# Row maxima of the attention scores by way of DRAM instead of TensorE

## The chip, the cores and the metric

The kernel runs on one core of one Trainium2 chip. The metric is the time of one execution on the device in microseconds (us), the median of several runs. TensorE is PE here (PEld is its weight load), VectorE is DVE, ScalarE is ACT, GpSimd is POOL, and SyncE is SP, whose queue issues nearly all DMAs.

## The reference

One layer of a decoder trunk over 2048 positions of width 1024, all in float32. After a norm, one input projection feeds an mLSTM group of four heads and an attention group (MLA) of eight heads; one output projection joins them, and a feed-forward part of width 4096 follows. The change lies in the attention of the eight heads:

```python
sc = jnp.einsum('bhqd,bkhd->bhqk', qblk, kf) * scale      # 96 wide: 64 plain, 32 rotary
sc = jnp.where(kpos[None, :] <= qpos[:, None], sc, -jnp.inf)
p = jax.nn.softmax(sc, axis=-1)
out = jnp.einsum('bhqk,bkhd->bqhd', p, vf)
```

## The kernel before

The program works through four stages: norm and input projections with the mLSTM (up to about 520 us of the profile), attention (about 520 to 965), the output projection (from about 964), and the feed-forward part (to the end).

In attention each head `h` goes through four blocks `qb` of 512 queries. For every block there are two passes. The first, `maxima` (L1548), finds a maximum for each query: a single rough product of queries and keys per 128 queries and up to 512 keys (`mm`, L1569, tile `m`, 512 columns wide where no mask falls), a maximum over the keys on DVE (`red`, L1574 and L1576, tile `mp`), and one more reduction over the pieces (`top_`, L1595), which leaves a tile `mx` of 128 partitions by 4 columns: the maximum of query `128 j + p` on partition `p`, column `j`. The second pass, `step` (L1615), makes the scores transposed, keys on partitions and queries along the row, in three products (`scores`, L1623, through the helper lines L245 to L247, tile `S`), takes their exponential on ACT (L1633, L1637), forms the low part of it on DVE or POOL (L1641, tile `pl`), and multiplies with the values (L1654, L1652, L1657, tile `o`).

The maximum has to be subtracted from scores that lie with the queries along the row. That is done inside the product: queries and keys have 96 rows, and a 97th, partition 96 of the tiles `QK0` (even heads) and `QK1` (odd heads), holds the negated maximum beside the queries and 1 beside the keys. To bring the maxima from partitions onto that row, `rows_` (L1597) runs four matmuls per block with one column of `mx` as weights and a 128x128 identity as the moving operand (L1600, tile `mt`, 1 partition by 512), and `put` (L1602) copies that row with a factor of -1 from PSUM to partition 96 on ACT (L1603). The row of ones is loaded once per tile `QK` from the input `edge` (L1473).

The order of PE, ACT, DVE and POOL is fixed in advance. A planner (`Plan`, L125) takes every operation with an estimated duration, its dependencies, its buffers and a key of urgency, places them greedily in time, and the instructions are written and pinned in that order (`pin`, L255). The first score of a block depends on `o_m[h, qb]`, the operation that leaves the row on partition 96. The DMAs on SP's queue are not pinned; the framework orders them, and SP issues them strictly one after another, waiting in front of each for what it needs. In attention SP's queue carries the loads of the next heads' queries and keys (L1523, L1525), the values (L1538), and for every finished block the store of its output (L1737) and of its sums (L1738), the load of the sums across partitions (L1742) and the store of their reciprocals (L1748).

The names in the orders and rows below read: `m5_3_3_3` is head 5, block 3, queries 3, keys 3; `mx5_3` the maxima of head 5, block 3; `S5_2_5` the scores of head 5, block 2, key tile 5. The number after the last underscore counts buffers.

Of the kernel before, what the change touches and what calls it, by code (L numbers as in the profile page):

```python
# [10 lines left out]
F32 = mybir.dt.float32  # L11
F32R = mybir.dt.float32r
I32 = mybir.dt.int32
BF16 = mybir.dt.bfloat16
AF = mybir.ActivationFunctionType
# [3 lines left out]
P = 128  # L19
SEQ = 2048  # L20
DM = 1024
KD = DM // P
TB = 512
# [4 lines left out]
NH = 8  # L28
# [9 lines left out]
TB_ = 1  # L38
TR_ = 1
EARLY = ()  # L40
EKEY = -165.0
EGAP = 1.5
LOL = 20.0
# [77 lines left out]
def f32(ap):  # L121
    return ap.bitcast(F32)
# [114 lines left out]
def trunk(ctx: ExitStack, tc: tile.TileContext, x, xT, pos, wu, wout, wup, wdn, cols, rows, consts, edge, out, dbg=None):  # L237
# [3 lines left out]
    vec, act, pool, pe = nc.vector, nc.scalar, nc.gpsimd, nc.tensor  # L241
    dma = nc.sync.dma_start
# [26 lines left out]
    dram = ctx.enter_context(tc.tile_pool(name="dram", bufs=1, space=DRAM))  # L269
# [16 lines left out]
    trep = [dram.tile([P, 2, TB], F32, tag=f"trep{b}", name=f"trep{b}") for b in range(NB)]  # L286
    trigd = dram.tile([64, SEQ], F32, tag="trigd", name="trigd")
    sumd = dram.tile([NH, SEQ], F32, tag="sumd", name="sumd")
    recd = dram.tile([NH, SEQ], F32, tag="recd", name="recd")
    x1d = out  # L290
    x1Td = dram.tile([DM, SEQ // 2], F32, tag="x1Td", name="x1Td")
# [4 lines left out]
    pl = Plan()  # L296
# [1110 lines left out]
    a2 = av = ar2 = pq = pS = po = onecol = maskneg = maskb = identb = None  # L1407
    pm = []
    QK, Qh, Ql, Kh, Kl = ([None, None] for _ in range(5))
# [42 lines left out]
    o_s1 = pl.op("Z", 0, switch1, pl.groups["e2"], -KEYA)  # L1452
    o_s2 = pl.op("Z", 0, switch2, unit_ops + [o_s1], -KEYA)
    o_s3 = pl.op("Z", 0, switch3, pl.groups["in"] + [o_s2], -KEYA)
    pl.group = "prep"
    for name, bufs, when in (
        ("q", 1, o_s1), ("m", 2, o_s2), ("S", SB_, o_s3), ("o0", 1, o_s3), ("o1", 1, o_s3), ("t", TB_, o_s3), ("th", 1, o_s3), ("tl", 1, o_s3), ("ph", HB_, o_s3), ("p", 1, o_s3), ("pl", LB_, o_s3), ("ot", 1, o_s3), ("ou", 1, o_s3),
        ("mp", 4, o_s1), ("mx", 2, o_s1), ("rsm", 2, o_s3),
    ):
        pl.ring(name, bufs, when)  # L1460

# [18 lines left out]
    blocks, first, start_of = [], {}, {}  # L1480
# [32 lines left out]
    o_kr, o_k, o_q, o_m, o_sc, o_pv, o_v = {}, {}, {}, {}, {}, {}, {}  # L1513
# [34 lines left out]
    def maxima(h, qb, keys):  # L1548
        s = h % 2
        mp = {}  # L1550
        reds = []

        def ring(i):
            return "q" if (h, qb) in EARLY or i % 3 == 2 else "m"

        def bank(i, name):
            return (pq if ring(i) == "q" else pm[0]).tile([P, TB], F32, tag=ring(i), name=name)

        def piece(j, kb, key):
            n = TB if kb < qb else (j + 1) * P  # L1560
            t = {}
            i = len(reds)

            def mm():
                if "t" not in mp:
                    mp["t"] = a2.tile([P, 4, 4], F32, tag="mp", name=f"mp{h}_{qb}", bufs=4)
                q0 = qb * TB + j * P
                t["p"] = ps = bank(i, f"m{h}_{qb}_{j}_{kb}")
                pe.matmul(ps[:, :n], Qh[s][0:96, q0 : q0 + P], Kh[s][0:96, kb * TB : kb * TB + n], start=True, stop=True)  # L1569

            def red():
                ps = t["p"]
                if kb < qb:
                    vec.tensor_reduce(mp["t"][:, j, kb : kb + 1], ps, axis=AX.X, op=ALU.max)  # L1574
                else:
                    vec.tensor_tensor_reduce(  # L1576
                        out=ps[:, :n], in0=ps[:, :n], in1=maskneg[:, 512 - n :], op0=ALU.add, op1=ALU.max, scale=1.0, scalar=NEG,
                        accum_out=mp["t"][:, j, kb : kb + 1],
                    )

            head = not reds
            a = pl.op("PE", n / 2.4 + (56 if n == P else 15), mm, [o_q[h, qb][0], o_k[h, kb][0], o_kr[s, kb], o_const[s]], key, take=(ring(i), "mp") if head else (ring(i),))
            if head:
                mp["op"] = a
            reds.append(pl.op("DVE", n / 0.96 + (148 if kb < qb else 285), red, [a, o_mask] if head else [a, o_mask, mp["op"]], key - 3, free=[(ring(i), a)]))

        todo = [(j, kb) for j in range(4) for kb in range(qb + 1)]
        for (j, kb), key in zip(todo, keys):
            piece(j, kb, key)
        t = {}  # L1590
        key = keys[-1] - 3

        def top_():
            t["m"] = a2.tile([P, 32], F32R, tag="mx", name=f"mx{h}_{qb}")[:, 0:4]
            vec.tensor_reduce(t["m"], mp["t"][:, :, 0 : qb + 1], axis=AX.X, op=ALU.max)  # L1595

        def rows_():  # L1597
            t["p"] = bank(len(reds), f"mt{h}_{qb}")
            for j in range(4):
                pe.matmul(t["p"][0:1, j * P : (j + 1) * P], t["m"][:, j : j + 1], identr, start=True, stop=True)  # L1600

        def put():  # L1602
            act.activation(Qh[s][96:97, qb * TB : (qb + 1) * TB], t["p"][0:1], AF.Copy, scale=-1.0)  # L1603

        a = pl.op("DVE", 80, top_, reds, key, take=("mx",), free=[("mp", mp["op"])])
        b = pl.op("PE", 4 * 75, rows_, [a, o_const[s]], key, take=(ring(len(reds)),), free=[("mx", a)])
        war = [o_sc[n] for n, (hh, q, _) in enumerate(blocks) if (hh, q) == (h - 2, qb)]
        o_m[h, qb] = pl.op("Activation", 585, put, [b] + war, key, free=[(ring(len(reds)), b)])

    acc, totals, tiles_of, lows = {}, {}, {}, []  # L1610
# [163 lines left out]

    early = [x for x in EARLY for _ in range(4 * x[1] + 4)]
    for i, x in enumerate(early):
# [26 lines left out]
    n = GT * P  # L1803
# [829 lines left out]
    for c in range(NCH):  # L2633
        ws = []
        for e in range(2):
            p = 2 * c + e
# [23 lines left out]
def prepare(inputs):  # L2660
    a = {k: np.asarray(v) for k, v in inputs.items()}
    x = np.ascontiguousarray(a["x"].reshape(SEQ, DM))
    w = a["w_in"][0]

    def unit(c):
        return c.reshape(KD, P, P).transpose(1, 0, 2).reshape(P, KD * P)

    kr = w[:, 1928:1960]
    z = np.zeros((DM, 56), np.float32)
    misc = np.concatenate([w[:, 1536:1544], z, kr, kr[:, 16:], kr[:, :16]], axis=1)  # L2670
    us = [unit(misc)]
    us += [unit(w[:, i * P : (i + 1) * P]) for i in range(4)]
    v = w[:, 512:1024].reshape(4, 2, P, 512)
    us += [v[j].transpose(1, 0, 2).reshape(P, 1024) for j in range(4)]
    us += [unit(w[:, 1024 + i * P : 1024 + (i + 1) * P]) for i in range(4)]
    us += [unit(w[:, 1544 + i * P : 1544 + (i + 1) * P]) for i in range(3)]
    ukv = a["w_ukv"][0].reshape(P, NH, 128)
    us.append(np.concatenate([ukv[:, :, :64].reshape(P, 512), ukv[:, :, 64:].reshape(P, 512)], axis=1))
    uq = a["w_uq"][0].reshape(2, P, NH, 96)
    us.append(uq[..., :64].reshape(2, P, 4, P).transpose(1, 2, 0, 3).reshape(P, 1024))  # L2680
    rope = uq[..., 64:].reshape(2, P, 2, 4, 2, 16).transpose(1, 2, 0, 4, 3, 5).reshape(P, 512)
    us.append(np.concatenate([rope, np.zeros((P, 512), np.float32)], axis=1))
    wu = np.ascontiguousarray(np.stack(us))
    wup = np.ascontiguousarray(a["w_up"][0].reshape(KD, P, DFF // P, P).transpose(2, 1, 0, 3).reshape(DFF // P, P, DM))

    def cv(v):
        return v.reshape(-1, P).T

    conv = a["conv_w"][0].reshape(4, 4, P).transpose(2, 1, 0).reshape(P, 16)
    cols = np.concatenate(  # L2690
        [conv, cv(a["conv_b"][0]), cv(a["norm_pre_mix"][0]), cv(a["ml_head_norm"][0]), cv(a["q_norm"][0]), cv(a["kv_norm"][0])], axis=1
    )
    rows = np.concatenate([a["b_gates"][0], a["norm_post_mix"][0], a["norm_pre_mlp"][0], a["norm_post_mlp"][0]])[None]
    consts = np.zeros((P, K_N), np.float32)
    consts[:, K_ID : K_ID + P] = np.eye(P)
    r = np.arange(P)
    consts[:, K_MASK + 384 : K_MASK + 512] = np.where(r[None, :] <= r[:, None], 0.0, NEG)
    consts[:, K_MASKT : K_MASKT + P] = np.where(r[None, :] >= r[:, None], 0.0, NEG)
    inv = np.array(INV_FREQ_BITS, np.uint32).view(np.float32)
    consts[:, K_INV] = inv[r % 16]  # L2700
    consts[:, K_NOT] = r != 64
    consts[:, K_OFF] = np.array([0.25, 0.25, 0.5, 0.0])[(r % 64) // 16]
    return {
        "x": x,
        "xT": np.ascontiguousarray(x.T),
        "pos": np.ascontiguousarray(a["positions"].reshape(1, SEQ)),
        "wu": wu,
        "wout": np.ascontiguousarray(a["w_out"][0]),
        "wup": wup,
        "wdn": np.ascontiguousarray(a["w_down"][0]),  # L2710
        "cols": np.ascontiguousarray(cols),
        "rows": np.ascontiguousarray(rows),
        "consts": consts,
        "edge": np.stack([np.ones(SEQ, np.float32), np.zeros(SEQ, np.float32)]),
    }


# [20 lines left out]
```

## Time and profile before

| | before |
|---|---|
| median of 3 runs | 2419.19 us (2416.09 to 2419.89) |
| profiled execution, its own time | 2418.22 us |
| its span in the trace | 2415.7 us |
| granted TensorE clock, mean | 0.994 |
| matmuls in the trace | 11135 |
| matmuls at L1600 (tile `mt`) | 128, 4 for each of 32 blocks |
| row copies at L1603 | 32, median 586 ns |

The span is what the trace covers, from the first instruction to the last; 2.5 us of the execution's time lie around it. A matmul's row gives its start and a duration; successive matmuls overlap, so how much time one takes from PE is read from the distance between starts. A line of a timeline gives the start in us, the duration in us, engine, source line, operation, result and operands, shape, and in brackets the idle time ahead of it with what ended it. SPq is SP's queue; its rows are issues of DMAs, not their landing. A line of waits reads: engine and line, then who was waited for, then the total in us, the number of times, and the longest one.

### The profile page before, as it was taken

Reading aid. Unit: us, or ns where it says so; the run is one execution under the profiler, and the core shown is the slowest. Engines: PE = TensorE matmul, PEld = TensorE weight load, DVE = VectorE, ACT = ScalarE, POOL = GpSimd, SP = SyncE. Lnnn points to the kernel's source line nnn. Section 1 sums busy time; section 2 is a strip of 40 time slices with the busy share of each in tenths; the row PEclk is TensorE's granted clock in tenths of the full one; section 3 lists DMA queues with packets and bytes.
Section 4 is the critical chain, followed back from the end, with each engine's and each line's share of the span. In section 5 each row is a group of like instructions: output and inputs, shape, how many; then the busy total and the mean of one; then the engine's idle time right before and its main releaser. Section 6 shows DMA issues by size and latency. Waiting matters only on the chain.

```text
span 2415.7 us, 34327 instructions
## 1 busy us (share of the span) xinstructions
PE 2372.5 (98%) x11135; PEld 1907.3 (79%) x11135; DVE 1722.8 (71%) x3125; ACT 1363.1 (56%) x2646; POOL 814.0 (34%) x697
## 2 busy tenths in 40 slices
PE   9999999999999999999999999999999999999997
PEld 7787777777777777788888888888888888888885
DVE  6865665658888887646866687766675677676778
ACT  5645454437788777544666556755665343443454
POOL 2634343428888888432000000000000322322346
PEclk9999999989999999999999999999999999999999
DMA  7697979887222321567877697755664435445448
GB/s 280 219 320 229 336 239 337 271 208 168 72 57 54 80 60 26 157 202 249 258 213 227 195 327 225 210 171 166 184 214 144 159 127 183 129 136 169 133 136 167
DMA packets 341308, 449.21 MB, mean 186 GB/s; under 512 B 34908, under 2 KB 227432, under 8 KB 341128
## 3 DMA queue, kind: packets, MB, share of 16 engines
q1 hardware_dynamic: 337192, 440.16, 58.6%
q0 software_dynamic: 3936, 6.87, 2.0%
q8 instruction: 87, 1.43, 0.2%
q14 instruction: 93, 0.76, 0.1%
HBM read 295.97 MB, written 153.05 MB: 186 GB/s over the span
## 4 chain that ended last, share of the span: by engine, by line
PE 53%; DVE 1%; DMA 1%; issue 0%; ACT 0%; SPq 0%; POOL 0%; DVEq 0%; ACTq 0%; POOLq 0%
PE op L245 1%; PE op L246 1%; PE op L247 1%; PE d_4X L2510 1%; PE d_3X L2512 1%; PE d_5X L2512 1%; PE d_4X L2512 1%; PE d_1X L2512 1%; PE d_1X L2511 1%; PE d_2X L2511 1%; PE d_3X L2511 1%; PE d_2X L2512 1%; PE d_4X L2511 1%; PE d_5X L2511 1%; PE d_5X L2510 1%; PE d_1X L2510 1%
## 5 line engine op out<-in xcount | busy, mean ns | idle before, releaser
L2548 POOL TENSOR_TENSOR y<-vd_0X,y 128x512 f32<-128x512 f32 x7 | 10.3, 1475 | 726.1 <-ACT vd_0X L2545 726.1
L1668 POOL TENSOR_TENSOR t<-t,ph 128x512 f32<-128x512 f32 (+1 forms) x192 | 213.0, 1110 | 17.8 <-ACT ph L1633 7.4
L1633 ACT ACTIVATE ph<-S 128x512 fp32r<-128x512 f32 (+1 forms) x320 | 170.4, 533 | 84.2 <-PE S L247 51.7
L2460 ACT CAST hh<-hr 128x512 fp32r<-128x512 f32 (+1 forms) x208 | 116.3, 567 | 156.1 <-DMA hr<-hd 15.3
L1641 DVE TENSOR_TENSOR pl<-S,ph 128x512 fp32r<-128x512 f32 (+3 forms) x272 | 157.1, 589 | 33.1 <-ACT S L1637 30.2
L245 PE MATMUL mm<-xh,wh 128*128 128x512 f32 x384 | 157.2, 409 | 5.4 <-ACT vs L813 1.9
L2465 DVE TENSOR_TENSOR hl<-hr,hh 128x512 fp32r<-128x512 f32 (+1 forms) x208 | 133.0, 647 | 30.2 <-ACT hh L2460 23.9
L246 PE MATMUL mm<-xl,wh 128*128 128x512 f32 x384 | 151.3, 394 | 0.9 <-DVE xl L416 0.9
L247 PE MATMUL mm<-xh,wl 128*128 128x512 f32 x384 | 151.1, 393 | 0.5 <-DVE wl L491 0.5
L1574 DVE TENSOR_REDUCE mp<-m 128x1 f32<-128x512 f32 x192 | 128.7, 681 | 19.1 <-PE m L1569 18.4
L1637 ACT ACTIVATE S<-S 128x512 f32<-128x512 f32 (+3 forms) x272 | 140.8, 518 | 0.4
L245 PE MATMUL S<-QK 97*128 97x512 f32 (+1 forms) x320 | 121.3, 379 | 2.4 <-DVE pl L1641 2.3
L1654 PE MATMUL o<-ph,V 128*128 128x512 f32 (+1 forms) x320 | 118.9, 378 | 2.2 <-DVE ot L1727 1.8
L1569 PE MATMUL m<-QK 96*128 96x512 f32 (+3 forms) x320 | 117.7, 400 | 1.3 <-DVE mp L1576 0.6
L246 PE MATMUL S<-QK 97*128 97x512 f32 (+1 forms) x320 | 118.2, 369 | 0.0
L247 PE MATMUL S<-QK 97*128 97x512 f32 (+1 forms) x320 | 117.8, 368 | 0.0
L1657 PE MATMUL o<-pl,V 128*65 128x512 f32 (+1 forms) x320 | 115.6, 362 | 0.6 <-POOL pl L1641 0.5
L245 PE MATMUL op<-wo,hh 128*128 128x512 f32 x256 | 101.0, 395 | 0.3 <-DVE osm L1958 0.2
L2299 ACT ACTIVATE t<-t 128x512 f32<-128x512 f32 x96 | 60.6, 632 | 70.8 <-DVE t L2294 70.1
L247 PE MATMUL op<-wo,hl 128*128 128x512 f32 x256 | 99.9, 390 | 0.0
L246 PE MATMUL op<-wo,hh 128*128 128x512 f32 x256 | 99.8, 390 | 0.0
L245 PEld LDWEIGHTS mm<-xh,wh 128*128 128x128 f32 x384 | 72.5, 189 | 26.9 <-ACT vs L813 2.4
(6451 smaller groups left out, 7485.9 us busy)
## 6 DMA issues: line engine op xcount, KB each, us to landing
hr<-hd SPq DMA_DIRECT2D x100, 448.0 KB
wr<-in_wu_dram SPq DMA_DIRECT2D x71, 512.0 KB
hd<-t SPq DMA_DIRECT2D x128, 256.0 KB
hd<-ts SPq DMA_DIRECT2D x96, 256.0 KB
wl<-wparts SPq DMA_DIRECT2D x45, 512.0 KB
QK<-qkd SPq DMA_DIRECT2D x32, 512.0 KB
xt<-in_x_dram SPq DMA_DIRECT2D x28, 512.0 KB
xf<-xd SPq DMA_DIRECT2D x40, 256.0 KB
```

Of the source, the lines that this page charges most:

```text
L245: pe.matmul(o, ah, bh, start=start, stop=False)
L246: pe.matmul(o, ah, bl, start=False, stop=False)
L247: pe.matmul(o, al, bh, start=False, stop=stop)
L1574: vec.tensor_reduce(mp["t"][:, j, kb : kb + 1], ps, axis=AX.X, op=ALU.max)
L1633: act.activation(t["h"][:, :w], t["S"][:, :w], AF.Exp)
L1637: act.activation(t["p"][:, :w], t["S"][:, :w], AF.Exp)
L1641: (pool if by_pool else vec).tensor_tensor(t["l"][:, :w], t["p"][:, :w], f32(t["h"][:, :w]), ALU.subtract)
L1654: pe.matmul(o0, v[:, 0:128], t["h"][:, :w], start=start, stop=stop)
L1668: pool.tensor_tensor(to, to, hv, ALU.add)
L2465: vec.tensor_tensor(t["l", m][:, :w], t["r", m][:, :w], f32(t["h", m][:, :w]), ALU.subtract)
L2511: pe.matmul(ps, a, w[:, 1], start=False, stop=False, skip_group_check=True)
L2512: pe.matmul(ps, b, w[:, 0], start=False, stop=stop, skip_group_check=True)
```

## The change

For heads 1 to 7 (`h >= MROW`, with `MROW = 1`) `rows_` and `put` go. In their place stand two DMAs on SP's queue per block. `lay` writes the 128x4 tile `mx` to a new DRAM tensor `mrowd`, 4 bytes at a time, so that the 512 maxima lie in a row; `fetch` reads that row of 2 KB back onto partition 96 of the tile `QK`. `fetch` waits for `lay` to land and for the scores of the block two heads earlier that read the same row. Head 0 keeps the matmuls and the copy. Since a DMA doesn't negate, the copy of head 0 loses its factor too, and the keys' row is loaded as -1 instead of 1. The tile `mx` has three buffers instead of two. In the planner, the two DMAs stand as two operations of SP (500 ns each to issue, then its fixed landing time).

```diff
-        ("mp", 4, o_s1), ("mx", 2, o_s1), ("rsm", 2, o_s3),
+        ("mp", 4, o_s1), ("mx", 3, o_s1), ("rsm", 2, o_s3),
...
         def put():
-            act.activation(Qh[s][96:97, qb * TB : (qb + 1) * TB], t["p"][0:1], AF.Copy, scale=-1.0)
+            act.activation(Qh[s][96:97, qb * TB : (qb + 1) * TB], t["p"][0:1], AF.Copy)
+
+        def lay():
+            dma(mrowd[h, qb * TB : (qb + 1) * TB].rearrange("(j p) -> p j", p=P), f32(t["m"]))
+
+        def fetch():
+            dma(f32(Qh[s][96:97, qb * TB : (qb + 1) * TB]), mrowd[h : h + 1, qb * TB : (qb + 1) * TB])
 
         a = pl.op("DVE", 80, top_, reds, key, take=("mx",), free=[("mp", mp["op"])])
+        war = [o_sc[n] for n, (hh, q, _) in enumerate(blocks) if (hh, q) == (h - 2, qb)]
+        if h >= MROW:
+            b = pl.op("SP", 500, lay, [a], key, free=[("mx", a)], kb=128)
+            o_m[h, qb] = pl.op("SP", 500, fetch, [b] + war, key, kb=64)
+            return
         b = pl.op("PE", 4 * 75, rows_, [a, o_const[s]], key, take=(ring(len(reds)),), free=[("mx", a)])
-        war = [o_sc[n] for n, (hh, q, _) in enumerate(blocks) if (hh, q) == (h - 2, qb)]
         o_m[h, qb] = pl.op("Activation", 585, put, [b] + war, key, free=[(ring(len(reds)), b)])
...
-        "edge": np.stack([np.ones(SEQ, np.float32), np.zeros(SEQ, np.float32)]),
+        "edge": np.stack([-np.ones(SEQ, np.float32), np.zeros(SEQ, np.float32)]),
```

On PE the 28 groups of four matmuls are gone, and since the planner places everything anew, other instructions of attention change their order a little as well. Where the row of head 5, block 3 was turned, PE had this before:

```order
L245 MATMUL S5_2_5_9380<-QK1_5248 128x512
L246 MATMUL S5_2_5_9380<-QK1_5248 128x512
L247 MATMUL S5_2_5_9380<-QK1_5248 128x512
L1600 MATMUL mt5_3_9390<-identr_63,mx5_3_9376 1x128 x4
L1569 MATMUL m6_0_3_0_9398<-QK0_4840 128x512
L1654 MATMUL o0_5_2_9361<-ph5_2_11_9336,V1_5246 128x128
```

and now has this (the source lines are two to twelve numbers higher in the changed file):

```order
L246 MATMUL S5_2_5_9305<-QK1_5249 128x512
L247 MATMUL S5_2_5_9305<-QK1_5249 128x512
L248 MATMUL S5_2_5_9305<-QK1_5249 128x512
L1571 MATMUL m6_0_3_0_9313<-QK0_4841 128x512
L1666 MATMUL o0_5_2_9283<-ph5_2_11_9256,V1_5247 128x128
```

Only the group of four has left this place. From the last product of this block's maxima (`m5_3_3_3`) to the first score that needs the row (`S5_3_0`) there were 65 rows on PE and there are 63 now. For the third blocks (`qb` = 3) of heads 1 to 7 that distance was 65, 85, 65, 65, 65, 83 and 53 rows, and is 65, 95, 81, 71, 63, 71 and 79.

SP's queue had the following around the same time: the sums and the output of head 5, block 1, their reload, and loads of the next queries.

```order
L1738 DMA sumd_74<-ou5_1_9330 1x512
L1748 DMA recd_75<-rsm5_0_9297 128x4
L1737 DMA hT_64<-ot5_1_9319 64x512
L1742 DMA rsm5_1_9448<-sumd_74 128x4
L1525 DMA QK1_5248<-qrd_66 16x2x512
L1748 DMA recd_75<-rsm5_1_9448 128x4
```

Now the two pairs for head 5, block 3 and head 6, block 0 stand among them:

```order
L1750 DMA sumd_74<-ou5_1_9250 1x512
L1760 DMA recd_76<-rsm5_0_9217 128x4
L1749 DMA hT_64<-ot5_1_9239 64x512
L1608 DMA mrowd_75<-mx5_3_9300 128x4x1
L1754 DMA rsm5_1_9373<-sumd_74 128x4
L1611 DMA QK1_5249<-mrowd_75 1x512
L1608 DMA mrowd_75<-mx6_0_9363 128x4x1
L1611 DMA QK0_4841<-mrowd_75 1x512
L1527 DMA QK1_5249<-qrd_66 16x2x512
L1760 DMA recd_76<-rsm5_1_9373 128x4
```

The first `lay` stands behind the store of an output that POOL has to finish, and its `fetch` has only the reload of the sums (`rsm5_1`) between itself and `lay`.

More of the change, by code (lines that the diff above doesn't have):

```diff
@@ L40 @@
 EARLY = ()
+MROW = 1
 EKEY = -165.0
@@ L288, in trunk @@
     sumd = dram.tile([NH, SEQ], F32, tag="sumd", name="sumd")
+    mrowd = dram.tile([NH, SEQ], F32, tag="mrowd", name="mrowd")
     recd = dram.tile([NH, SEQ], F32, tag="recd", name="recd")
@@ L1593, in top_ @@
         def top_():
-            t["m"] = a2.tile([P, 32], F32R, tag="mx", name=f"mx{h}_{qb}")[:, 0:4]
+            t["m"] = a2.tile([P, 32], F32R, tag="mx", name=f"mx{h}_{qb}", bufs=3)[:, 0:4]
             vec.tensor_reduce(t["m"], mp["t"][:, :, 0 : qb + 1], axis=AX.X, op=ALU.max)
```

## The prediction

> **What bounds the kernel now.** The page comes first: which engine is full over the whole span.
>
> ```profile
> span 2415.7 us, 34327 instructions
> PE 2372.5 (98%) x11135; PEld 1907.3 (79%) x11135; DVE 1722.8 (71%) x3125; ACT 1363.1 (56%) x2646; POOL 814.0 (34%) x697
> ```
>
> PE is busy for 98% of the span, but the average says nothing of attention by itself. So next the table by stretches, for 600 to 955 us, where heads 1 to 7 run undisturbed, and with it what PE waited for there:
>
> ```profile
> core 0: us, PE busy (x) PEld busy (x) DVE busy (x) ACT busy (x) POOL busy (x), PEclk, DMA share, GB/s
> 600.00:955.00 355.00, 350.33 (x1812) 268.66 (x1812) 300.98 (x675) 279.03 (x581) 293.13 (x254) 1.00 0.24 57
> PE S L245 <- DVE pl L1641: 1.6, 3, 0.8
> PE o L1654 <- DVE ot L1727: 1.5, 4, 0.7
> PE o L1680 <- POOL tl L1676: 0.9, 2, 0.8
> ```
>
> PE is busy for 350.33 of 355 us at the full granted clock (1.00). Its listed waits come to 4.0 us. DVE (301 us), POOL (293) and ACT (279) all have room, and the DMA engines are busy for 24%. In this stage PE sets the pace, so time taken off PE should come off the end, and SP's queue has bandwidth to spare; what has to be asked of SP is latency and order.
>
> **What is removed.** The tile `mt` in the trace:
>
> ```profile
> L1600 PEld LDWEIGHTS mt<-identr,mx x128: 79/83/123, 521.5 to 956.5; 128*1 128x1 f32 x128
> L1600 PE MATMUL mt<-identr,mx x128: 218/223/309, 521.5 to 956.6; 128*1 128x128 f32 x128
> L1603 ACT ACTIVATE QK<-mt x32: 584/586/587, 521.9 to 957.0; 1x512 fp32r<-1x512 f32 x32
> ```
>
> Of 128 matmuls, 4 x 28 = 112 go, and 28 of 32 copies. A median of 223 ns for each matmul would make 112 x 0.223 = 25 us, but these durations overlap. The timeline of PE shows what one group really takes, here in the middle and at the end of attention:
>
> ```profile
> 844.23 0.39 PE L245 MATMUL S<-QK 97*128 97x512 f32 x1
> 844.47 0.39 PE L246 MATMUL S<-QK 97*128 97x512 f32 x1
> 844.69 0.39 PE L247 MATMUL S<-QK 97*128 97x512 f32 x1
> 844.92 0.40 PE L1600 MATMUL mt<-identr,mx 128*1 128x128 f32 x4
> 845.16 0.45 PE L1569 MATMUL m<-QK 96*128 96x512 f32 x1
> 845.45 0.23 PE L1654 MATMUL o<-ph,V 128*128 128x128 f32 x1
> ...
> 956.39 0.40 PE L1600 MATMUL mt<-identr,mx 128*1 128x128 f32 x4
> 956.63 0.45 PE L245 MATMUL S<-QK 97*128 97x512 f32 x1
> 956.92 0.39 PE L246 MATMUL S<-QK 97*128 97x512 f32 x1
> ```
>
> A product of 512 columns starts 0.23 us after the one ahead of it (844.23, 844.47, 844.69, 844.92). The four short ones take 0.24 us together (844.92 to 845.16), and the product behind them takes 0.29 instead of 0.23 (845.16 to 845.45; 956.63 to 956.92), so 0.06 us more go there. One group costs 0.24 + 0.06 = 0.30 us; over 28 groups about 28 x 0.29 = **8.1 us**. The Trainium skill ("Trainium Kernel Development and Optimization", Performance Expectations) calls the busy time of matmuls a bad metric, since matmuls are pipelined; this trace agrees, 0.24 us between starts against 4 x 0.223 us of durations, and by the durations the sum would have been 25 us.
>
> ACT loses 28 x 0.586 = 16.4 us, 6% of its work there. It is not the bound, so I count nothing for it; at most it removes some of PE's waits on `pl`, which hangs on ACT's exponentials, and with it a part of the 4.0 us above. The changed sign is another constant in the same load and a copy without a factor: nothing. The planner's new order moves other rows of attention, but their work is the same.
>
> **What is added: the way through DRAM.** Per block one row of latency on SP's queue, in place of PE and ACT. Its parts, by the nearest rows:
>
> ```profile
> 826.86 0.39 SPq L1738 DMA_DIRECT2D sumd<-ou  x1
> 827.36 1.18 SPq L1525 DMA_DIRECT2D QK<-qrd  x2
> 828.63 0.53 SPq L1742 DMA_DIRECT2D rsm<-sumd  x1
> 1006.76 0.38 SPq L1742 DMA_DIRECT2D rsm<-sumd  x1
> 1009.14 0.18 DVE L1745 RECIPROCAL rsm<-rsm 128x4 f32<-128x4 f32 x1 [0.69 <-DMA rsm<-sumd]
> L1850 SPq DMA_DIRECT2D gcol<-in_rows_dram x1: 385/385/385, 994.5 to 994.5; - x1
> DMA packets 1089, 0.22 MB, mean 155 GB/s; under 512 B 1037, under 2 KB 1037, under 8 KB 1089
> ```
>
> A store of a 2 KB row (`sumd`) and the load that reads it back: the load is issued 1.77 us after the store's issue began, so the store had landed by then. A small load (`rsm`) has DVE waiting for it until 2.38 us after its issue began (1006.76 to 1009.14). `lay` has no row of its own: 512 elements of 4 bytes each. The nearest is `gcol`, 1024 elements of 4 bytes; nearly all of its packets (1037 under 512 B, in the DMA view for 996.4 to 997.8) moved within 1.4 us, so 512 take about 0.7 us. I take 1.77 + 0.7 = 2.5 us for `lay` and 2.4 us for `fetch`: 4.9 us from `lay`'s issue to the row on partition 96. Ends: 3.5 us if both are like the quick store, 7.0 us if elements of 4 bytes are stored at a quarter of the rate at which `gcol`'s were loaded (0.7 becomes 2.8).
>
> What covers this is the time from `mx` to the block's first score. It is shortest for the third blocks, here heads 1 and 5, with the store of an output that stands ahead of `lay` on SP's queue:
>
> ```profile
> 616.97 0.15 DVE L1595 TENSOR_REDUCE mx<-mp 128x4 fp32r<-128x16 f32 x1
> 616.93 0.48 SPq L1737 DMA_DIRECT2D hT<-ot  x1
> 625.41 0.40 PE L245 MATMUL S<-QK 97*128 97x512 f32 x1
> 843.30 0.15 DVE L1595 TENSOR_REDUCE mx<-mp 128x4 fp32r<-128x16 f32 x1
> 844.81 0.48 SPq L1737 DMA_DIRECT2D hT<-ot  x1
> 845.39 0.54 SPq L1742 DMA_DIRECT2D rsm<-sumd  x1
> 847.50 0.15 DVE L1595 TENSOR_REDUCE mx<-mp 128x4 fp32r<-128x4 f32 x1
> 851.16 0.55 SPq L1525 DMA_DIRECT2D QK<-qrd  x1
> 851.87 0.39 PE L245 MATMUL S<-QK 97*128 97x512 f32 x1
> ```
>
> In head 5 `lay` goes out when the store's issue ends, at 845.3; the row lies at 850.2; the first score starts at 851.87, less 2 rows of the new order (0.4 us), at 851.5. Spare: 1.3 us. In head 1 `lay` goes out at 617.5, the row lies at 622.4, the score is due at 625.4: 3.0 us. Heads 2, 3, 4, 6 and 7 have 71 to 95 rows between the last product of the maxima and the first score, where these two have 63 and 65; at 0.23 us for a full product, 6 rows are another 1.4 us or so: about 4.4 us for heads 4 and 6, 6 and more for 2, 3 and 7. The other blocks (`qb` 0 to 2) start their maxima earlier still. So the sum holds **0** for the new waits; if the 4.9 are 7.0, head 5 is late by 0.8 us and no other: +1 us.
>
> Queued behind a waiting `fetch` on SP: in head 5 the pair for head 6, block 0, whose `mx` is ready at 847.65 and which has a whole block's time until it is needed, and the loads of queries for head 7. In the trace SP issues nothing there from 845.9 to 851.16, so they fit. `mx` has a third buffer, and the closest two of these rows are 4.2 us apart (843.30 and 847.50), so three take well over 4.9 us and DVE doesn't wait for `lay`. At the end of attention `fetch` of head 7, block 3 stands ahead of a reload for the output projection; with 79 rows it goes out in time.
>
> A rule of the Trainium skill speaks against `lay` ("DMA: Bandwidth & Descriptors", Rules for kernel authors): a strided last dimension is cut into one descriptor per element, and a transpose by a plain DMA with a rearranged pattern is given as 19 times as costly as the hardware's. If that held for the whole store, 19 x 1.77 = 34 us, it would make an estimate of 28 x 34 = 940 us of waiting on SP; `gcol`'s packets, 1024 elements in 1.4 us, agree with a descriptor per element but not with that price here.
>
> Sum: 2418.2 - 8.1 = 2410.1 us for the profiled execution. It ran 1.0 us below the median of the runs, so on the median's footing **2411 us**.
>
> **The rivals.**
>
> *Late rows* (slower). If `lay` and `fetch` together take about 12 us instead of 4.9, the first scores stall PE, which has nothing else to run in its fixed order. At 12 us, 7.1 more than summed, what is left after the spare above is 5.8 in head 5, 4.1 in head 1, 2.7 each in heads 4 and 6 and about 0.7 each in 3 and 7: 17 us, so 2411 + 17 = 2428. It decides from about 10 us on, where the lateness reaches the 8.1 us gained. For it: 4-byte stores to DRAM have no row in this trace. Against: twice the price of the nearest rows is needed. Chance 0.09.
>
> *The store at the rule's price* (much slower): SP blocked for 28 x 34 = 950 us in a stage of 435 us (521.5 to 956.5 in the rows of `mt`), so 2411 + 515 = 2926. `gcol` speaks against it. Chance 0.01.
>
> *The other engines take it back* (no change). PE's 355 us have DVE at 301 and POOL at 293 beside them; the waits on `pl`, `ot` and `tl` above double or triple when PE arrives 2% earlier, by 4 to 6 us: 2415 to 2417. For it: all of PE's waits are of this kind. Against: 15% of DVE is free, and ACT, ahead of it, gets lighter. Chance 0.18.
>
> *More than PE's own work goes*: ACT's 16.4 us shorten the chain ahead of `pl` and PE's 4.0 us of waits disappear: 2411 - 4 = 2407. Chance 0.07.
>
> That the change doesn't do what it says can be left out: PE has 28 rows fewer, ACT 28 fewer, and 56 DMAs are new.
>
> **How the numbers follow.** The forecast, 2411 with 2409 to 2414, has 0.65. No change that a measurement of this kernel can tell is 0.2%, 4.8 us, so above 2414.4 and below 2424. Faster: 0.65 and 0.07 less a little at the edge, 0.72. Same: the engines that take it back, 0.18. Slower: the late rows and the rule's price, 0.10. The range reaches down to 2406, below the case of more, since the runs of before themselves spread over 3.8 us, and up to 2419, over the case of no change; outside lie the slower cases and a few hundredths at either end.
>
> **What would show it.** Right: 16 matmuls at `mt` and 4 copies left; busy PE in attention down by about 8 us and the whole attention stage shorter by as much; no wait of PE on a DMA of `QK` from `mrowd` above 1 us; `fetch` issued some 2.5 us after `lay`. Wrong: waits of PE at the first scores of third blocks named after that DMA (late rows); waits of PE on `pl`, `ot` and `tl` well above 4.0 us with the stage hardly shorter (the other engines). A gain that appears in attention and is gone after it would mean a stage behind it that waits for DMAs, which nothing above shows.

## The result, and the profile after

| | before | after |
|---|---|---|
| median of the runs | 2418.77 us (2416.09 to 2419.89, 4 runs) | 2477.59 us (2474.15 to 2478.68, 4 runs) |
| ratio to before, with its 95% interval | 1 | 1.0242 [1.0225, 1.026] |
| span of the profiled execution | 2415.7 us | 2472.4 us |
| first score of head 7, block 3 | 961.79 us | 1020.69 us |
| distance from `lay` to `fetch` on SP, 28 blocks | none | 7.85 to 12.65 us, median 9.4 |

The change makes the kernel slower by 2.4%; the forecast of 2411 us was 66.6 us too low. All of the loss arises in attention: its last block begins 58.9 us later, and from there to the end both kernels take about the same. The matmuls and copies went as announced (16 and 4 are left at `mt`). From the page of the kernel after, and its table by stretches, from the first score of head 1 to that of head 7:

```profile
span 2472.4 us, 34188 instructions
PE 2389.0 (97%) x11023; PEld 1913.4 (77%) x11023; DVE 1716.9 (69%) x3125; ACT 1347.2 (54%) x2618; POOL 815.3 (33%) x697
...
595.25:987.93 392.68, 349.83 (x1633) 264.29 (x1632) 283.33 (x644) 252.81 (x529) 278.08 (x239) 0.92 0.31 61
```

And the same stretch of the kernel before, between the same two scores:

```profile
592.46:931.21 338.75, 334.49 (x1729) 256.22 (x1728) 286.81 (x645) 266.33 (x555) 279.90 (x241) 1.00 0.26 62
```

PE runs 96 matmuls fewer (24 groups of four), yet the stretch is 53.9 us longer. Two things are new. PE is idle for 392.68 - 349.83 = 42.9 us instead of 4.3. And it is busy for longer with less work: 349.83 us for 1633 matmuls against 334.49 for 1729, at a granted clock of 0.92 instead of 1.00.

What each engine waited for in attention in the kernel after (560 to 1025 us), PE's list first, then DVE's, then SP's (total us, times, longest):

```profile
PE S L246 <- DMA QK<-mrowd: 12.8, 4, 4.9
PE S L246 <- DVE pl L1653: 9.2, 8, 5.7
PE o L1666 <- DVE ot L1739: 7.2, 3, 6.1
PE m L1571 <- DVE mp L1576: 6.1, 1, 6.1
PE S L246 <- DVE mp L1578: 3.4, 1, 3.4
...
DVE rsm L1757 <- DMA rsm<-sumd: 43.4, 15, 7.1
DVE ou L1743 <- DMA sumd<-ou: 5.1, 1, 5.1
...
SPq L1611 <- DMA mrowd<-mx: 172.0, 24, 10.8
```

The first line is the late row itself. The other four of PE name DVE, and DVE's own list tells why: it waits 43.4 us for the reload of the sums (`rsm`), which is no part of the change, and once 5.1 us for the store of the sums. SP's queue stands 172 us in front of `fetch`, waiting for `lay`. In the kernel before, DVE's wait for the reload was this:

```profile
DVE rsm L1745 <- DMA rsm<-sumd: 0.7, 1, 0.7
```

One such place on SP's queue and on PE, head 4, block 3, with the view of DMA packets from 817.8 to 819.2 us between them, and last the table by stretches for 828.46 to 835.29 us:

```profile
817.72 0.37 SPq L1608 DMA_DIRECT2D mrowd<-mx  x1
819.97 0.47 SPq L1749 DMA_DIRECT2D hT<-ot  x1
820.54 0.54 SPq L1754 DMA_DIRECT2D rsm<-sumd  x1
825.89 0.23 SPq L1611 DMA_DIRECT2D QK<-mrowd  x1
...
DMA packets 530, 0.00 MB, mean 3 GB/s; under 512 B 529, under 2 KB 529, under 8 KB 530
...
826.37 0.44 PE L1669 MATMUL o<-pl,V 128*65 128x512 f32 x1 [0.64 <-POOL pl L1653]
829.17 0.77 PE L246 MATMUL S<-QK 97*128 97x512 f32 x1 [2.36 <-DMA QK<-mrowd]
829.73 0.63 PE L247 MATMUL S<-QK 97*128 97x512 f32 x1
830.16 0.63 PE L248 MATMUL S<-QK 97*128 97x512 f32 x1
...
828.46:835.29 6.83, 6.12 (x15) 4.58 (x16) 1.53 (x4) 2.03 (x4) 1.01 (x2) 0.50 0.03 3
```

`lay` is issued at 817.72. Its 512 small packets have moved by 819.2, in the time that the prediction gave them. But `fetch`, which waits for `lay` to land, goes out only at 825.89, 8.2 us after `lay`. The row's first user starts at 829.17 after 2.36 us of waiting, and the products behind it follow at distances of 0.43 us (829.73 to 830.16) instead of 0.23, at a granted clock of 0.50.

### The profile page after: what moved, and what is told of

Same layout as the page of the kernel before. It is cut to its first block, busy times and chain, and to the rows that moved or that the text cites. A ratio compares the mean times of both kernels' runs of the same rounds, so it can differ in the third digit from the quotient of the medians.

```text
span 2472.4 us, 34188 instructions
## 1 busy us (share of the span) xinstructions
PE 2389.0 (97%) x11023; PEld 1913.4 (77%) x11023; DVE 1716.9 (69%) x3125; ACT 1347.2 (54%) x2618; POOL 815.3 (33%) x697
## 4 chain that ended last, share of the span: by engine, by line
PE 81%; DMA 9%; DVE 5%; issue 2%; ACT 2%; POOL 1%; SPq 1%; DVEq 0%; POOLq 0%; ACTq 0%
PE mm L246 3%; PE mm L248 3%; PE mm L247 3%; DMA rsm<-sumd 3%; PE op L247 2%; PE op L246 2%; PE op L248 2%; DMA mrowd<-mx 2%; PE S L246 2%; PE o L1666 2%; PE m L1571 2%; PE o L1669 2%; PE S L247 2%; PE S L248 2%; PE mv L246 1%
## 5 line engine op out<-in xcount | busy, mean ns | idle before, releaser
L246 PE MATMUL S<-QK 97*128 97x512 f32 (+1 forms) x320 | 127.2, 398 | 26.6 <-DMA QK<-mrowd 12.8
L247 PE MATMUL S<-QK 97*128 97x512 f32 (+1 forms) x320 | 121.7, 380 | 0.0
L248 PE MATMUL S<-QK 97*128 97x512 f32 (+1 forms) x320 | 121.4, 379 | 0.0
L246 PEld LDWEIGHTS S<-QK 97*128 97x128 f32 x320 | 64.2, 201 | 49.7 <-DVE pl L1653 17.9
```

The source lines that it names most:

```text
L246: pe.matmul(o, ah, bh, start=start, stop=False)
L247: pe.matmul(o, ah, bl, start=False, stop=False)
L248: pe.matmul(o, al, bh, start=False, stop=stop)
```

## The experiments

Three theories stood at the start. **A**: stores of 4-byte elements to DRAM land 8 to 12 us after their issue, and everything else follows. **B**: any round trip through DRAM for which SP's queue stands waiting has this effect. **C**: the new order of the engines lost cover that the old one had. Every ratio below is to runs of the kernel before made beside the run in question (their medians: 2416.97 to 2419.19 us).

### The store alone, and the store on another queue

The kernel before keeps its matmuls and copies, and stores `mx` beside them; nobody reads the store. `mx` has three buffers here, as in the change.

```diff
+        def lay():
+            dma(mrowd[h, qb * TB : (qb + 1) * TB].rearrange("(j p) -> p j", p=P), f32(t["m"]))
...
+        if h:
+            pl.op("SP", 500, lay, [a], key, free=[("mx", a)], kb=128)
```

> The kernel before with its matmuls and copies, and lay as in the change beside them (4-byte stores for heads 1 to 7), which nobody reads or waits for. If only the waits of fetch and of the first scores cost time, this is 2419 us (2416 to 2423). If a slow store also holds up what SP issues behind it on the same queue (landing late), DVE waits for rsm as in the changed kernel and the time is 2435 us or more.

Measured: 2463.29 us, ratio 1.0195 [1.0181, 1.0209]. A store without a reader costs 46 us, so most of the loss doesn't come from late rows. How it reaches PE, at one place of this kernel, on SP's queue, on DVE and on PE:

```profile
890.83 0.56 SPq L1607 DMA_DIRECT2D mrowd<-mx  x1
891.49 0.46 SPq L1748 DMA_DIRECT2D rsm<-sumd  x1
...
901.79 0.18 DVE L1751 RECIPROCAL rsm<-rsm 128x4 f32<-128x4 f32 x1 [4.72 <-DMA rsm<-sumd]
902.46 0.68 DVE L1647 TENSOR_TENSOR pl<-S,ph 128x512 fp32r<-128x512 f32 x1
...
899.32 0.40 PE L1570 MATMUL m<-QK 96*128 96x512 f32 x1
903.20 0.50 PE L245 MATMUL S<-QK 97*128 97x512 f32 x1 [3.48 <-DVE pl L1647]
903.53 0.39 PE L246 MATMUL S<-QK 97*128 97x512 f32 x1
903.76 0.45 PE L247 MATMUL S<-QK 97*128 97x512 f32 x1
904.01 0.63 PE L1570 MATMUL m<-QK 96*128 96x512 f32 x1
904.44 0.63 PE L1660 MATMUL o<-ph,V 128*128 128x512 f32 x1
```

The reload of the sums, issued 0.66 us behind the store, reaches DVE only 10.3 us after its issue. DVE works in its fixed order, so it stands 4.72 us at the reciprocal; PE then stands 3.48 us for a `pl` that is queued behind the reciprocal. The next products come 0.23 and 0.25 us apart, and from 904.01 on 0.43 us apart (904.01 to 904.44).

In the other kernel `lay` of the change is issued from ACT's queue instead of SP's:

```diff
-            dma(mrowd[h, qb * TB : (qb + 1) * TB].rearrange("(j p) -> p j", p=P), f32(t["m"]))
+            act.dma_start(mrowd[h, qb * TB : (qb + 1) * TB].rearrange("(j p) -> p j", p=P), f32(t["m"]))
```

> The changed kernel with lay issued from ACT's queue instead of SP's; fetch stays on SP and still waits for lay. lay's landing stays at 8 us or more by theory A. If the loss comes mostly from what lands late behind lay on its own queue, DVE's waits for rsm shrink to a few us and the time falls to about 2440 us; if it comes from SP standing still at fetch and from late rows, the time stays at 2465 us or more. By theory C nothing changes: 2477 us.

Measured: 2490.64 us, ratio 1.0305 [1.0291, 1.0319]: no better than on SP. PE's waits in this kernel, and DVE's for the reload of the sums:

```profile
PE o L1666 <- DVE ot L1739: 20.9, 6, 7.0
PE S L246 <- DMA QK<-mrowd: 19.7, 4, 7.1
...
DVE rsm L1757 <- DMA rsm<-sumd: 40.4, 12, 5.8
```

The reloads go out on SP's queue, `lay` on ACT's, and DVE's wait is about what it was (40.4 against 43.4 us). So what is late beside `lay` is late on whichever queue `lay` was issued.

### The same way through DRAM in larger runs

Here DVE turns `mx` in 32x32 pieces first, so that `lay` stores 128 runs of 128 bytes and `fetch` reads 16 runs of 128 bytes.

```diff
+                vec.transpose(f32(t["x"]), f32(mcol))
...
-            dma(mrowd[h, qb * TB : (qb + 1) * TB].rearrange("(j p) -> p j", p=P), f32(t["m"]))
+            dma(mrowd[h, qb], f32(t["x"]))
```

> The maxima are turned in 32x32 blocks on DVE first, so that the store writes 128 runs of 128 bytes and the load reads 16 such runs; the two DMAs, their place on SP and the row on partition 96 stay. Theory A (stores of 4-byte elements land late, after 8 to 12 us, and the stalls follow from that): fetch is issued 2 to 3 us after lay, PE no longer waits at the first scores, about 2411 us (2409 to 2415). Theory B (any round trip through DRAM that SP has to wait for costs this): fetch still stands 5 us or more behind lay or DVE still waits for rsm, above 2440 us. Theory C (the new order of the engines lost the cover, whatever the DMA): the order is nearly the same here, so 2450 us or more.

Measured: 2414.61 us, ratio 0.9989 [0.998, 0.9998]. SP's wait in front of `fetch` in this kernel, against 172.0 us in the change:

```profile
SPq L1616 <- DMA mrowd<-mx: 17.8, 17, 2.3
```

In the second kernel `lay` stores each partition's four maxima as one run of 16 bytes, and the 4-byte elements are on the reading side.

```diff
-            dma(mrowd[h, qb * TB : (qb + 1) * TB].rearrange("(j p) -> p j", p=P), f32(t["m"]))
+            dma(mrowd[h, qb * TB : (qb + 1) * TB].rearrange("(p j) -> p j", p=P), f32(t["m"]))
...
+                mrowd[h : h + 1, qb * TB : (qb + 1) * TB].rearrange("o (p j) -> o j p", j=4),
```

> lay stores runs of 16 bytes (128 of them), fetch does the turning and reads 512 elements of 4 bytes out of DRAM into the row. Theory A says that it is the store's 4-byte elements: fetch 2 to 3 us after lay; the load of small elements costs under 1 us more than a load of 2 KB, so 2411 to 2418 us. If small elements are as slow on the side of the load, first scores are late again and the time is 2440 us or more. Theory B: above 2440 us as well, with fetch 5 us or more behind lay.

Measured: 2416.63 us, ratio 0.9997 [0.9988, 1.0006]. Both keep the round trip; the second has the very order of the change, the first nearly, since its turn is more work for DVE. The loss is gone in both: B and C fall as its cause. Loading 512 elements of 4 bytes does no such harm; storing them as the change does is what costs.

### Is it the small element, their number, or that they touch?

All of these are the kernel before with an unread store, as above; only the store's pattern differs. First, 128 runs of 16 bytes, and one column of `mx` (128 elements of 4 bytes, side by side) instead of four:

```diff
-            dma(mrowd[h, qb * TB : (qb + 1) * TB].rearrange("(j p) -> p j", p=P), f32(t["m"]))
+            dma(mrowd[h, qb * TB : (qb + 1) * TB].rearrange("(p j) -> p j", p=P), f32(t["m"]))
...
+            dma(mrowd[h, qb * TB : qb * TB + P].rearrange("(j p) -> p j", p=P), f32(t["m"][:, 0:1]))
```

> The kernel before, with its matmuls and copies, and beside them a store of every mx of heads 1 to 7 to DRAM in 128 runs of 16 bytes, which nobody reads: the control of the store in 512 elements of 4 bytes that made 2463.3 us (46 us above before). If it is the small element that lands late and holds up what is issued behind it, this one costs next to nothing: 2415 to 2421 us. If any extra store of mx on SP's queue, at these 28 places, holds up the others, it is near 2463 as well.

> As the unread store of 4-byte elements (2463.3 us), but of one column of mx instead of four: 128 elements of 4 bytes, side by side in DRAM. If the time to land goes with the number of elements (512 take some 8 us longer than a quick store, so 128 some 2 us), most of the loss goes: 2417 to 2428 us. If it is a fixed time of any store with elements of 4 bytes, it stays near 2463 us.

Measured: 2422.45 us, 1.0017 [1.0008, 1.0027], for runs of 16 bytes, and 2451.22 us, 1.0134 [1.0115, 1.0153], for one column. An extra store as such, with the order that it brings, costs some 4 us, a little above the 2415 to 2421 that were expected. A quarter of the elements keeps about two thirds of the loss, so the loss doesn't go with the number of elements, nor is it fixed: neither expectation for the one column (2417 to 2428, or near 2463) held.

Then 512 elements again, but apart from each other in DRAM: by 512, 64, 16 and 8 bytes.

```diff
-    mrowd = dram.tile([NH, SEQ], F32, tag="mrowd", name="mrowd")
+    mrowd = dram.tile([NH, SEQ, 128], F32, tag="mrowd", name="mrowd")   # 16, 4 and 2 in the others
...
-            dma(mrowd[h, qb * TB : (qb + 1) * TB].rearrange("(j p) -> p j", p=P), f32(t["m"]))
+            dma(mrowd[h, qb * TB : (qb + 1) * TB, 0].rearrange("(j p) -> p j", p=P), f32(t["m"]))
```

> As the unread store of 4-byte elements (2463.3 us), but in DRAM the elements lie 512 bytes apart instead of side by side. Theory A1, each small element has its price whatever lies beside it: the same as there, 2455 to 2475 us. Theory A2, the price comes from neighbouring elements that fall into the same stretch of DRAM and wait for one another (each is read, changed and written back): the cost goes, 2415 to 2425 us. Between the two: part of each.

> The kernel before, with the unread store in 4-byte elements 64 bytes apart: 2422 us as with 512 bytes apart (2422.3) if 64 bytes are enough, up to 2430 if not.

> The kernel before, with the unread store in 4-byte elements 16 bytes apart, so that four instead of sixteen of them share 64 bytes. If the time to land goes with the number of elements that share a stretch, a quarter of the 41 us between side by side (2463.3) and 512 bytes apart (2422.3) is left: 2428 to 2436 us. If only elements that touch one another wait, 2422 us; if the stretch matters and not the number in it, near 2463 us.

> The kernel before, with the unread store in 4-byte elements 8 bytes apart. 16 bytes apart made 2423.3 us, side by side 2463.3. If elements hold each other up only where they touch, 2423 us; if where two or more share 16 bytes, part or all of the 40 us: 2432 to 2463 us.

| distance of 4-byte elements | median | ratio to before |
|---|---|---|
| 4 bytes (side by side) | 2463.29 us | 1.0195 [1.0181, 1.0209] |
| 8 bytes | 2426.26 us | 1.0031 [1.0018, 1.0043] |
| 16 bytes | 2423.29 us | 1.0017 [1.0008, 1.0026] |
| 64 bytes | 2424.26 us | 1.0021 [1.0012, 1.0031] |
| 512 bytes | 2422.30 us | 1.002 [1.001, 1.0029] |

The number and the size of the elements are the same in each row. Where 4-byte elements touch, the store costs about 40 us more than with any gap; with a gap of only 4 bytes, some 4 more than with the widest gap. This last result lies between the two that were expected for it (2423, or 2432 to 2463). Touching alone doesn't do it: the runs of 16 bytes touch one another too, and cost no more than the elements 512 bytes apart. DVE's wait for the reload of the sums, in the kernels with four columns and with one column side by side, then 8 and 512 bytes apart:

```profile
DVE rsm L1751 <- DMA rsm<-sumd: 34.3, 9, 7.1
```

```profile
DVE rsm L1751 <- DMA rsm<-sumd: 28.0, 10, 5.8
```

```profile
DVE rsm L1751 <- DMA rsm<-sumd: 5.9, 5, 1.9
```

```profile
DVE rsm L1751 <- DMA rsm<-sumd: 1.9, 1, 1.9
```

And the same place as above, with 512 bytes between the elements, on SP's queue and on DVE:

```profile
863.99 0.57 SPq L1607 DMA_DIRECT2D mrowd<-mx  x1
864.65 0.45 SPq L1748 DMA_DIRECT2D rsm<-sumd  x1
...
870.38 0.17 DVE L1751 RECIPROCAL rsm<-rsm 128x4 f32<-128x4 f32 x1
```

The same two DMAs, 0.66 us apart as before, and DVE finds the sums there when its turn comes. The Trainium skill ("DMA: Bandwidth & Descriptors", Specifications) states that a transfer under 512 bytes makes the engine read, change and write back. By that alone all five rows of the table would be alike; the runs don't agree, since 4 bytes each at a distance of 16 are quick. What in the memory makes touching elements wait is shown by no run here.

### The change with its elements apart

The changed kernel itself, with `lay` writing and `fetch` reading elements 512 or 64 bytes apart; in a third kernel head 0 goes that way too (`MROW = 0`).

```diff
-    mrowd = dram.tile([NH, SEQ], F32, tag="mrowd", name="mrowd")
+    mrowd = dram.tile([NH, SEQ, 16], F32, tag="mrowd", name="mrowd")   # 128 for 512 bytes
...
+            dma(mrowd[h, qb * TB : (qb + 1) * TB, 0].rearrange("(j p) -> p j", p=P), f32(t["m"]))
...
+            dma(f32(Qh[s][96:97, qb * TB : (qb + 1) * TB]), mrowd[h : h + 1, qb * TB : (qb + 1) * TB, 0])
```

> The changed kernel, with the 512 elements of lay 512 bytes apart in DRAM instead of side by side, and fetch reading them from there. Theory A2, the late landing comes from 4-byte elements that lie side by side in DRAM: fetch goes out 1.4 to 5 us after lay as in the other quick stores, PE waits for no row, and what is left of the sum's 8.1 us is what the transposed store kept (2414.6 us) or a little more, since nothing is added on VectorE: 2410 to 2417 us. Rival, a store of 4-byte elements lands late wherever they lie, and the unread one 512 bytes apart was harmless only because nobody waited for it: fetch 8 us and more after lay, about 17 us of late rows, 2425 to 2435 us.

> As the kernel with 512 bytes between the elements, with 64 bytes. If elements hold each other up only within 64 bytes or less, the same as there, 2410 to 2417 us. If they do so within 512 bytes, there are 8 in each such stretch instead of 128 (1 for the wide spacing), and a sixteenth of the loss would be left, about 4 us: 2414 to 2422 us.

> The changed kernel with elements 64 bytes apart (2412.9 us), and head 0 by way of DRAM as well, so that no group of four matmuls is left. By the sum another 4 x 0.29 = 1.2 us on PE, if head 0's first scores, which come 8 to 12 us after its maxima, leave 4.9 us for the way: 2411 to 2413 us. If the start of attention, with its loads of keys and values on the same queue, makes its rows late: 2414 to 2425 us.

Measured: 2413.86 us, ratio 0.998 [0.9971, 0.9989], with 512 bytes; **2412.94 us, 0.9979 [0.9969, 0.9988], with 64 bytes**; 2416.74 us, 0.9996 [0.9987, 1.0005], with head 0 as well. The middle one is the fastest kernel of this study, 6.05 us below the 2418.99 us of before beside it, and 64.7 us below the change, from which it differs in nothing but the layout of a scratch tensor. Its stretch from the first score of head 1 to that of head 7, SP's wait in front of `fetch`, DVE's for the reload of the sums, and head 5, block 3 on SP's queue:

```profile
591.37:924.71 333.34, 328.80 (x1633) 250.80 (x1632) 284.86 (x645) 253.33 (x531) 279.93 (x241) 1.00 0.33 68
...
SPq L1611 <- DMA mrowd<-mx: 30.9, 19, 3.7
...
DVE rsm L1757 <- DMA rsm<-sumd: 0.8, 2, 0.6
...
839.44 0.54 SPq L1608 DMA_DIRECT2D mrowd<-mx  x1
840.09 0.48 SPq L1754 DMA_DIRECT2D rsm<-sumd  x1
841.96 0.53 SPq L1611 DMA_DIRECT2D QK<-mrowd  x1
```

In this place `fetch` goes out 2.5 us after `lay`, just what the prediction had given it. In 22 of the 28 blocks the distance is 2.05 to 4.91 us; in the other six, where the store of an output that has to wait for POOL stands between the two on SP's queue, it is 7.66 to 8.66, and PE waits for no row there either. With head 0 on this way too, the second range held: its first score comes at 534.33 us instead of 530.77, so the start of attention loses more than the last four groups gave.

### More cover

The planner is told of 7 us more between `lay` and `fetch`, so it moves the maxima ahead; once with the change's store, once with elements 64 bytes apart.

```diff
             b = pl.op("SP", 500, lay, [a], key, free=[("mx", a)], kb=128)
+            b = pl.op("X", 7000, lambda: None, [b], key)
             o_m[h, qb] = pl.op("SP", 500, fetch, [b] + war, key, kb=64)
```

> The changed kernel, with the planner told of 7 us more between lay and fetch, so that it moves the rows of the maxima ahead: the first scores of the third blocks get 75 to 107 rows of cover instead of 63 to 95. The stores are the same. If the late rows themselves are only the smaller part of the loss (some 17 us of PE's waits at first scores, the rest at DMAs behind lay that land late), it keeps most of it: 2452 to 2466 us. If the late rows are the whole of it, it comes down to 2411 to 2420 us.

> The kernel whose planner moves the rows of the maxima ahead (2500.9 us, more than the 2477.6 it should have mended), with the elements of lay 64 bytes apart. If its loss came from the stores and from what waits behind them, with the order itself harmless, it comes down to the kernel with 64 bytes apart and the old order (2412.9): 2411 to 2419 us. If the earlier rows themselves made it worse (other engines' orders, buffers held longer), a good part of the 23 us stays: 2425 to 2437 us.

Measured: 2500.93 us, 1.0343 [1.0328, 1.0359], and 2424.99 us, 1.0024 [1.0014, 1.0034]. Neither range of the first expectation held; the second result lies at the lower end of its worse range (2425 to 2437). No PE wait for a row is left among the long ones, yet the kernel is 23 us slower than the change, and DVE waits longer for the reloads than ever. DVE's wait in the first, then in the second:

```profile
DVE rsm L1758 <- DMA rsm<-sumd: 51.4, 11, 10.7
```

```profile
DVE rsm L1758 <- DMA rsm<-sumd: 1.7, 1, 1.7
```

With the second kernel the two parts come apart: the earlier maxima cost 2424.99 - 2412.94 = 12.1 us by themselves (through what is not followed up here), the touching elements 2500.93 - 2424.99 = 75.9 us in this order against 64.7 in the old one. Cover for the row is no remedy, because the row is not what most of the loss hangs on.

## Why the prediction was wrong, point by point

**What bounds the kernel, and what is removed.** Right. PE sets the pace, and with a harmless store the gain comes off the end. The size: over the stretch above, PE's 24 groups fewer make 338.75 - 333.34 = 5.41 us, 0.23 us a group. That is near the 0.24 us between starts; the 0.06 us on the product behind, which the sum had added (it wrote 0.30 and multiplied 0.29), didn't come back. 28 groups at that rate make 6.3 us, and 6.05 were measured at the end (2.9 to 7.5 by the interval of the ratio), where the sum had 8.1.

**What is added: the failed step.** The sum gave `lay` 1.77 + 0.7 = 2.5 us and at most 4.6, by the rate at which `gcol`'s 1024 small elements were loaded. The 0.7 us for the packets were near (818.2 to 819.0 in the place above), and so were the 2.5 us for elements that don't touch (2.05 to 4.91 where nothing else held `fetch` up). But `lay` of the change lands late, after its packets have moved: `fetch` goes out 7.85 to 12.65 us after it. A load's row was taken to bound a store's, and neither end of the range allowed the time between moving and landing to grow beyond that of a quick store.

**Queued behind a waiting `fetch`: "so they fit".** This looked at when SP could issue, not at when that which it issues near `lay` lands. It is the larger part of the miss: a store that nobody waits for costs 46 us (41 more than the same one 512 bytes apart), because reloads issued just behind it land late as well, and DVE meets them in a fixed order. The prediction's list of what would show it wrong named PE's waits on `mrowd`, `pl`, `ot` and `tl`; it had no line for DVE waiting on `rsm`, which turned out to be the longest wait of an engine on a DMA (43.4 us).

**The rival of late rows.** Its mechanism is there, and its size: with about 12 us for both DMAs it had 17 us, and PE's distances in front of five first scores (5.28, 2.80, 5.33, 3.85 and 0.93 us instead of 0.23, in heads 1, 4, 5, 6 and 7) are 17.0 too long in sum. In head 6 the trace names DVE for the wait (the 3.4 us at `mp` above), which had itself stood for a late reload; there `fetch` had gone out at 961.44, only 1.4 us ahead of the score. Without head 6 it is 13.4. Either way it is only the smaller part of the 66.6 us. The store at the rule's price, 950 us of SP, didn't come: SP stood 172.0 us for `lay`.

**What no step had: the clock.** The change and the kernel with elements 64 bytes apart run the same 1633 matmuls between the first scores of heads 1 and 7, in 392.68 and 333.34 us. Of the 59.3 us between them, (392.68 - 349.83) - (333.34 - 328.80) = 38.3 are idle time of PE, and 349.83 - 328.80 = 21.0 are slower matmuls: after a wait, products of 512 columns come 0.43 us apart instead of 0.23 for a while. The Trainium skill ("TensorE: Matmul & The Clock Gate", Part 1) states that PE's clock is halved after an idle window of about 3.4 us and comes back after as long a busy one. The trace agrees with the halving but not with an idle time of 3.4 us: in the place above it is in force from 828.46 us, 0.7 us before the end of a wait of 2.36 us, with one of 0.64 us shortly ahead of it. Taken together, the stalls cost about half as much again as their own length (21.0 us on 38.3).

**The other engines, and the planner's order.** With a harmless store nothing shows that DVE and POOL took anything back (6.05 us came of 6.3); the rival's price was loose too, since 4.0 us of waits that triple are 8 more, not 6. The order that the change brings costs nothing that can be seen, though another order can: 12.1 us with the maxima moved ahead.

## What to carry to other kernels

A DMA is priced by when it lands, not by when its packets have moved, and what counts is also what is issued around it: ask of each new store which loads go out within the next 10 us and which engine meets them in a fixed order. Here a load of small elements said nothing about a store of small elements. When 4-byte elements must be scattered to DRAM, put them 16 bytes apart or more, or make runs of 16 bytes, and read the profile for waits on DMAs that the change didn't touch.

## What the runs showed of the hardware that was not expected

- A store of 4-byte elements that touch in DRAM landed 8 to 12 us after its issue (the distance from `lay` to `fetch`), though in the place shown its 512 packets had moved within 1.5 us. With 16 to 512 bytes from element to element, or in runs of 16 or 128 bytes, no such lateness was seen, and with 8 bytes little of it (DVE's wait of 5.9 us instead of 1.9). 128 such elements cost 32 us of the kernel's time, 512 cost 46.
- What is issued behind such a store lands late with it: a 2 KB reload took over 10 us until DVE could go on (891.49 to 901.79). Issuing the store from another engine's queue didn't help (2490.64 us).
- Waits of 2.4 to 6 us in front of PE were followed by products at 0.43 us instead of 0.23 (granted clock 0.50 from 828.46 to 835.29 us), which made 21 of the 59 us lost in the stretch.
